# A tuned matmul with bias and tanh: the opening's loads in order of need, and the work of the first row tiles reordered

## The chip, the cores and the metric

One core of one Trainium2 chip. The metric is the time of one execution in microseconds (us), as the median of several runs. The span of a profiled execution is about 1.7 us shorter than its time (1780.2 us of 1781.94 for the kernel before).

## The reference

```python
def reference(a, b, bias):          # a, b: 4096 x 4096 float32; bias: 4096 float32
    return np.tanh(np.matmul(a, b) + bias)
```

## The kernel before

A row tile is 128 rows of A, a k-tile 128 of the inner dimension. A and B are cast to float16 as GpSimd's loads bring them in; TensorE multiplies 128 x 128 by 128 x 512. After a start the kernel runs as a plain loop in which TensorE never waits. The start is special, because A and B have to arrive while TensorE already works: eight row tiles (the first four are `g0`, the second four `g1`) are done together on parts of K, and partial sums are put aside in SBUF (`spill`) and added to later.

The opening (cut):

```python
fill(WARM, NB)                        # dummy matmuls on zeros, WARM = 11
raw_b = spill[3]...                   # float32 landing place of B's k-tiles 0 and 1
for t, copy in enumerate((nc.scalar.copy, nc.vector.tensor_copy)):
    load_b_low(nc.sync, raw_b[:, ds(t, 1), :], 0, t, 1)      # SyncE, 512 KB each
    copy(b_cur[0][:, t, :], raw_b[:, t, :])                  # rounding to float16
...
for m in g0:
    load_nat(m)                       # GpSimd: 128 x 512 of A, turned by TensorE
...
load_b_next()                         # B's k-tiles 2 and 3, GpSimd
load_b_next()
turn_nat(0, nc.vector.tensor_copy)    # four transposes and a copy out of PSUM
fill(3, P)
turn_nat(1, nc.scalar.copy)
row(0, 0, 2)                          # row tile 0, k-tiles 0 and 1: four matmuls
turn_nat(2, nc.vector.tensor_copy)
row(1, 0, 2)
...
```

The later loads are kept in a list and issued by GpSimd in this order, as far as three buffers for A allow (cut):

```python
want_a("g1a", 2, 4 * P, 2 * Q, 0, BL)      # row tiles 4, 5, k-tiles 0..3: four 64 KB loads
want_a("g1a2", 2, 6 * P, 2 * Q, 0, BL)     # row tiles 6, 7
want_a("g1b", G, 4 * P, G * Q, BL, BL)     # row tiles 4..7, k-tiles 4..7
for i in range(BL):
    want(load_b_next)                      # B's k-tiles 4..7
want_a("g0b", G, 0, G * Q, BL, BL)         # row tiles 0..3, k-tiles 4..7
want_a("g0c", G, 0, G * Q, KS, KM - KS)    # row tiles 0..3, k-tiles 8..15
...
```

And the end of the start, where the second four row tiles are finished and the first four take up their second half of K:

```python
for t in (KM, KM + 8):
    for i in range(G):
        turn(ats[G + i], ("g1", t), i * Q, t, 8)      # VectorE transposes
    for m in g1 if t == KM else g0:
        for j in range(J):
            add_bias(m, j)                            # VectorE, eight adds
    across(ps, g1, t, min(t + 8, KT - TB), KS)
turn(ats[0], ("g0", 0), 0, KM, KT - KM)               # row tile 0's second half
down(ps, g1, KT - TB, KT, end)                        # eight final adds, tanh, store
...
for m in g0:
    for j in range(J):
        ...                                           # 16 matmuls
        if m < G - 1 and j == 0:
            turn(ats[m + 1], ("g0", m + 1), 0, KM, KT - KM)
        ...
        end(ps, m, j)
```

## Time and profile before

| | before |
|---|---|
| time, median of 3 runs | 1781.81 us (1781.77 to 1782.02) |
| span of the profiled run | 1780.2 us |
| TensorE busy | 1774.4 us |
| first useful matmul | 7.44 us |
| start of the second four row tiles | 14.80 us |
| row tile 0's second half of K on VectorE | 85.07 us |
| plain loop starts (chain of waits) | 119.10 us |

How to read it: from 119.10 us on TensorE runs without a gap until the last 3.5 us. Whatever a change in the start does to that one number goes into the time one to one, and a load that comes late costs nothing as long as TensorE finds its data. The prediction below shows the lines.

### The profile page before, as it was taken

The page shows a single profiled execution, that of the slowest core. Times are in us where ns is not written, and L with a number is a line of the kernel's source. Part 1 is how long each engine was busy: PE and PEld are TensorE (multiplying, and loading weights), DVE is VectorE, ACT ScalarE, POOL GpSimd, SP SyncE. Part 2 cuts the span into 40 slices and gives each one's busy share as a digit, 9 for nine tenths or more (in the row PEclk, how much of TensorE's full clock was granted, in tenths as well). Part 3 has the DMA queues.
Part 4 walks back from the last instruction along what each step waited for, and adds up shares of the span by engine and source line. Part 5 has one row for each costly group of instructions (what it writes and reads, how often), then busy time and mean ns, then how long its engine had stood idle before and what let it go on. Part 6 is the DMA issues. An engine that isn't in the chain of part 4 may idle for free.

```text
span 1780.2 us, 20854 instructions
## 1 busy us (share of the span) xinstructions
PE 1774.4 (100%) x8254; PEld 806.9 (45%) x8254; DVE 763.8 (43%) x680; ACT 173.2 (10%) x279; POOL 872.1 (49%) x1618
## 2 busy tenths in 40 slices
PE   9999999999999999999999999999999999999999
PEld 4444444444444444444444444444444444444444
DVE  3764353444344443444344443444344443444342
ACT  2011000000000000000000000000000000000001
POOL 7465566544466554444456554444544454444510
PEclk9999999999999999999999999999999999999999
DMA  9999999976999877767699987766776667766641
GB/s 186 203 189 178 168 166 169 140 124 109 165 165 173 148 115 115 119 114 121 113 177 165 170 137 115 119 115 109 129 117 120 107 114 115 120 114 109 116 77 42
DMA packets 281393, 238.94 MB, mean 134 GB/s; under 512 B 159056, under 2 KB 231760, under 8 KB 281296
## 3 DMA queue, kind: packets, MB, share of 16 engines
q0 software_dynamic: 243280, 167.88, 70.1%
q1 hardware_dynamic: 37728, 69.62, 11.0%
q8 instruction: 64, 1.05, 0.2%
q14 instruction: 33, 0.27, 0.0%
q10 hardware_dynamic: 288, 0.13, 0.0%
HBM read 337.64 MB, written 67.11 MB: 227 GB/s over the span
## 4 chain that ended last, share of the span: by engine, by line
PE 99%; DMA 0%; issue 0%; ACT 0%; POOL 0%; DVE 0%; DVEq 0%; POOLq 0%
PE ps L412 93%; PE ps L138 6%; DMA nat<-in_a_dram 0%; ACT o_sb L152 0%; PE tp L257 0%; POOL nat L246 0%; DVE o_sb L149 0%; DVEq L149 0%; POOLq L435 0%
## 5 line engine op out<-in xcount | busy, mean ns | idle before, releaser
L412 PE MATMUL ps<-b,at 128*128 128x512 f16 x7712 | 1657.8, 378 | 0.0
L90 POOL DMA_DIRECT2D an<-in_a_dram x1492 | 805.5, 547 | 796.6 <-DVE at L100 583.4
L412 PEld LDWEIGHTS <-at 128*128 128x128 f16 x7712 | 754.6, 98 | 903.3
L100 DVE STREAM_TRANSPOSE at<-an 128x512 f16<-128x512 f16 (+1 forms) x380 | 565.6, 1539 | 85.8 <-DMA an<-in_a_dram 85.8
L149 DVE TENSOR_TENSOR o_sb<-ps,bias_bc 128x512 f32<-128x512 f32 (+1 forms) x243 | 165.4, 683 | 897.7 <-PE ps L412 695.7
L152 ACT ACTIVATE o_sb<-o_sb 128x512 f32<-128x512 f32 (+1 forms) x243 | 151.8, 626 | 1499.1 <-DVE o_sb L149 1499.1
L73 POOL DMA_DIRECT2D b<-in_b_dram x104 | 56.2, 544 | 15.5 <-DMA an<-in_a_dram 8.4
L138 PE MATMUL ps<-b,atx 128*128 128x512 f16 x256 | 56.2, 379 | 0.0
L138 PE MATMUL ps<-b,at 128*128 128x512 f16 x256 | 55.7, 379 | 0.1
L138 PEld LDWEIGHTS <-at 128*128 128x128 f16 x256 | 25.0, 98 | 30.5 <-DVE spill L181 0.5
L138 PEld LDWEIGHTS <-atx 128*128 128x128 f16 x256 | 24.6, 98 | 30.1 <-DVE atx L100 0.9
L100 DVE STREAM_TRANSPOSE atx<-an 128x512 f16<-128x512 f16 (+2 forms) x12 | 16.3, 1399 | 13.0 <-DMA an<-in_a_dram 13.0
L69 POOL DMA_DIRECT2D b<-in_b_dram x12 | 7.8, 654 | 22.4 <-PE ps L412 22.3
L152 ACT ACTIVATE spill<-spill 128x512 f32<-128x512 f32 x16 | 9.9, 632 | 85.6 <-DVE spill L149 85.5
L149 DVE TENSOR_TENSOR spill<-ps,spill 128x512 f32<-128x512 f32 x16 | 10.4, 678 | 9.9 <-PE ps L138 9.9
L181 DVE TENSOR_TENSOR spill<-spill,bias_bc 128x512 f32<-128x512 f32 x16 | 9.7, 680 | 0.0
L173 ACT COPY spill<-ps 128x512 f32<-128x512 f32 x16 | 8.0, 623 | 12.9 <-PE ps L138 12.9
L228 PE MATMUL ps<-zeros 128*128 128x512 f16 (+1 forms) x14 | 4.7, 498 | 1.3 <-DVE zeros L221 1.3
L176 DVE TENSOR_TENSOR spill<-ps,spill 128x512 f32<-128x512 f32 x8 | 4.8, 670 | 0.0
L228 PEld LDWEIGHTS <-zeros 128*128 128x128 f16 x14 | 1.6, 130 | 3.7 <-issue 2.4
L239 DVE CAST b<-spill 128x1024 f16<-128x1024 f32 x1 | 0.8, 849 | 4.5 <-DMA spill<-in_b_dram 4.5
L246 POOL DMA_DIRECT2D nat<-in_a_dram x4 | 2.3, 587 | 0.8 <-POOLq L435 0.8
(14 smaller groups left out, 8.9 us busy)
## 6 DMA issues: line engine op xcount, KB each, us to landing
an<-in_a_dram POOLq DMA_DIRECT2D x480, 192.0 KB, 5.1
out_dram<-o_sb SPq DMA_DIRECT2D x239, 256.0 KB, 2.7
an<-in_a_dram POOLq DMA_DIRECT2D x960, 32.0 KB, 2.7
b<-in_b_dram POOLq DMA_DIRECT2D x94, 256.0 KB, 8.2
b<-in_b_dram POOLq DMA_DIRECT2D x6, 1024.0 KB, 13.5
an<-in_a_dram POOLq DMA_DIRECT2D x32, 128.0 KB, 5.6
out_dram<-spill SPq DMA_DIRECT2D x16, 256.0 KB, 5.9
an<-in_a_dram POOLq DMA_DIRECT2D x12, 256.0 KB, 8.2
```

The source lines that it names most:

```text
L69: queue.dma_start(out=dst, in_=src[:, ds(t0 % BL, nt), :])
L73: nc.gpsimd.dma_start(out=bt[t0 // TB][ds(q * QP, QP), ds(t0 % TB, nt), :], in_=src.rearrange("(t p) n -> p t n", p=QP),)
L90: nc.gpsimd.dma_start(out=an[ds(q * QP, QP), :, ds((t - t0) * QP, n * QP)], in_=src.rearrange("(mb p) k -> p mb k", p=QP),)
L100: nc.vector.transpose(at[:, ds(t, n), :].rearrange("P t (mb p) -> P mb t p", p=QP), an[:, ds(mb0, Q), ds((t - t0) * QP, n * QP)].rearrange ...
L138: nc.tensor.matmul(ps, at[:, t, :], bt[t // TB][:, t % TB, ts(j, NB)], start=start, stop=stop)
L149: nc.vector.tensor_tensor(out=o_sb[:, piece], in0=ps[:, piece], in1=addend[:, piece], op=mybir.AluOpType.add)
L152: nc.scalar.activation(o_sb[:, piece], o_sb[:, piece], mybir.ActivationFunctionType.Tanh)
L173: nc.scalar.copy(aside(m, j), ps)
L176: nc.vector.tensor_tensor(out=aside(m, j), in0=ps, in1=aside(m, j), op=mybir.AluOpType.add)
L181: nc.vector.tensor_tensor(out=aside(m, j), in0=aside(m, j), in1=bias_bc[:, ts(j, NB)], op=mybir.AluOpType.add)
L228: nc.tensor.matmul(ps[:, ds(0, w)], zeros[:, :P], zeros[:, :w], start=i == 0, stop=i == n - 1)
L412: nc.tensor.matmul(ps, at[:, t, :], b_cur[t // TB][:, t % TB, ds(c0, w)], start=t == 0, stop=t == KT - 1,)
```

## The change

The intent: load first what TensorE needs first, so that the useful work starts earlier, and take VectorE's bias adds out of places where transposes are wanted. It has four parts, which I call the opening, the halves, the pairs and the adds. In the opening, the memset writes into the landing place of B's second k-tile, so SyncE's load of that tile has to wait for it, and it stands behind three loads on GpSimd. I call this the hold.

```diff
# the opening
-    WARM = 11
+    WARM = 9
-    for t, copy in enumerate((nc.scalar.copy, nc.vector.tensor_copy)):
-        load_b_low(nc.sync, raw_b[:, ds(t, 1), :], 0, t, 1)
-        copy(b_cur[0][:, t, :], raw_b[:, t, :])
+    load_b_low(nc.sync, raw_b[:, ds(0, 1), :], 0, 0, 1)
+    for j, copy in enumerate((nc.scalar.copy, nc.vector.tensor_copy)):
+        copy(b_cur[0][:, 0, ts(j, NB)], raw_b[:, 0, ts(j, NB)])
...   (copies of the transposed tiles out of PSUM in two halves each)
-    for m in g0:
+    for m in range(3):
         load_nat(m)
+    nc.gpsimd.memset(raw_b[:, 1, ds(0, 1)], 0.0)      # holds the next load back
+    load_b_low(nc.sync, raw_b[:, ds(1, 1), :], 0, 1, 1)
+    load_nat(3)
...
-    row(0, 0, 2)
+    nc.vector.tensor_copy(b_cur[0][:, 1, :], raw_b[:, 1, :])
+    row(0, 0, 1)
+    row(1, 0, 1)
+    fill(2, P)
     turn_nat(2, nc.vector.tensor_copy)
-    row(1, 0, 2)
+    row(0, 1, 1)
+    row(1, 1, 1)
# the halves
-    want_a("g0c", G, 0, G * Q, KS, KM - KS)
-    for u in range(KS, KM, 2):
-        want(lambda u=u: load_b_all(u, 2))
+    for t in (KS, KS + 4):
+        want_a(("g0", t), G, 0, G * Q, t, 4)
+        for u in (t, t + 2):
+            want(lambda u=u: load_b_all(u, 2))
# the pairs: B's k-tiles 16..19 and 24..27 by two and not by four, the bias load
# after B's k-tiles 24..27 and not before B's 16                     (cut)
# the adds
-        for m in g1 if t == KM else g0:
-            for j in range(J):
-                add_bias(m, j)
         across(ps, g1, t, min(t + 8, KT - TB), KS)
+    for m in g1:
+        for j in range(J):
+            add_bias(m, j)
     turn(ats[0], ("g0", 0), 0, KM, KT - KM)
     down(ps, g1, KT - TB, KT, end)
+    for m in g0:
+        for j in range(J):
+            add_bias(m, j)
```

More of the change, by code (lines that the diff above doesn't have):

```diff
@@ L257, in turn_nat @@
             nc.tensor.transpose(tp[:, t, :], nats[m][:, :, t], ident)
-        copy(ats[m][:, ds(0, BL), :], tp)
+        for t in range(0, BL, 2):
+            copy(ats[m][:, ds(t, 2), :], tp[:, ds(t, 2), :])
     nats, b_done = {}, [2]
-    for m in g0:
+    for m in range(3):
         load_nat(m)
+    nc.gpsimd.memset(raw_b[:, 1, ds(0, 1)], 0.0)
+    load_b_low(nc.sync, raw_b[:, ds(1, 1), :], 0, 1, 1)
+    load_nat(3)
     nc.gpsimd.affine_select(
@@ L300 @@
     bias_bc = biasp.tile([P, NCW], fp32, name="bias_bc")
-    want(lambda: load_bias(bias_bc, 0, nc.gpsimd))
     for t in (KM, KM + 8):
         want_a(("g1", t), G, 4 * P, G * Q, t, 8)
-        for u in range(t, t + 8, TB):
-            want(lambda u=u: load_b_all(u, TB))
+        for u in (t, t + 2):
+            want(lambda u=u: load_b_all(u, 2))
+        if t > KM:
+            want(lambda: load_bias(bias_bc, 0, nc.gpsimd))
+        want(lambda t=t: load_b_all(t + TB, TB))
     for m in g0:
@@ L325 @@
     ps = {}
-    for m in g0:
-        turn(ats[m], "g0c", m * Q, KS, KM - KS)
+    for t in (KS, KS + 4):
+        for m in g0:
+            turn(ats[m], ("g0", t), m * Q, t, 4)
     one_by_one(ps, g0, BL, KS, BL)
@@ L343 @@
             turn(ats[G + i], ("g1", t), i * Q, t, 8)
-        for m in g1 if t == KM else g0:
-            for j in range(J):
-                add_bias(m, j)
         across(ps, g1, t, min(t + 8, KT - TB), KS)
+    for m in g1:
+        for j in range(J):
+            add_bias(m, j)
     turn(ats[0], ("g0", 0), 0, KM, KT - KM)
     down(ps, g1, KT - TB, KT, end)
+    for m in g0:
+        for j in range(J):
+            add_bias(m, j)
     ahead = 3
```

## The prediction

> **What bounds the kernel now.** I read the page first, for the span and the busy shares; then the chain that ended last in order of time, for where TensorE's stream begins and breaks; then the timelines of single engines around the places that the change touches.
>
> The page of the kernel before, its first lines and a line of its chain:
>
> ```profile
> span 1780.2 us, 20854 instructions
> PE 1774.4 (100%) x8254; PEld 806.9 (45%) x8254; DVE 763.8 (43%) x680; ACT 173.2 (10%) x279; POOL 872.1 (49%) x1618
> ...
> PE 99%; DMA 0%; issue 0%; ACT 0%; POOL 0%; DVE 0%; DVEq 0%; POOLq 0%
> ```
>
> TensorE is the bound, but a busy share of 100% alone doesn't say that it runs at its pace, because matmuls are pipelined. A long stretch in the middle does, in the view by windows:
>
> ```profile
> 1000.00:1700.00 700.00, 700.00 (x3245) 317.38 (x3244) 297.82 (x254) 63.78 (x101) 328.91 (x614) 1.00 0.72 119
> ```
>
> 700 us over 3245 matmuls is 0.2157 us each, and there are 4096 x 4096 x 4096 / (128 x 128 x 512) = 8192 of that size: 8192 x 0.2157 = 1767 us that no ordering of loads changes. Of the span of 1780.2 only about 13 us are open to anything, and the chain in order of time shows where they lie:
>
> ```profile
> 7.11 0.05 issue
> 7.16 0.42 PE tp L257 x4
> 7.58 0.90 PE ps L138 x4
> 8.48 0.22 PE tp L257 x4
> 8.70 0.86 PE ps L138 x4
> 9.56 0.22 PE tp L257 x4
> 9.79 25.99 PE ps L138 x120
> 35.78 0.05 issue
> 35.82 41.60 PE ps L138 x192
> 77.42 0.08 issue
> 77.50 41.60 PE ps L138 x192
> 119.10 1654.20 PE ps L412 x7680
> ```
>
> The first useful matmul starts at 7.44 us, the transposes between rows cost 0.22 each, and afterwards the stream is without gaps but for 0.05 and 0.08 us. 120 x 0.2157 = 25.9 against 25.99, 192 x 0.2157 = 41.4 against 41.60. So all that the change can win is in the first 7.4 us, and every stall that it makes later is paid in full. The last 3.5 us (a last add, tanh and store) are not touched.
>
> Two later places have little slack. In VectorE's timeline, at 28 us and at 85 to 101 us:
>
> ```profile
> 27.93 2.50 DVE L100 STREAM_TRANSPOSE atx<-an 128x512 f16<-128x512 f16 x4 [6.30 <-DMA an<-in_a_dram]
> ...
> 46.16 2.37 DVE L100 STREAM_TRANSPOSE at<-an 128x1024 f16<-128x1024 f16 x2 [8.22 <-DMA an<-in_a_dram]
> 48.46 4.84 DVE L176 TENSOR_TENSOR spill<-ps,spill 128x512 f32<-128x512 f32 x8
> ```
>
> ```profile
> 85.07 2.31 DVE L100 STREAM_TRANSPOSE atx<-an 128x2048 f16<-128x2048 f16 x1 [3.85 <-DMA an<-in_a_dram]
> 87.31 4.90 DVE L149 TENSOR_TENSOR spill<-ps,spill 128x512 f32<-128x512 f32 x8
> 92.12 2.30 DVE L100 STREAM_TRANSPOSE atx<-an 128x2048 f16<-128x2048 f16 x1
> 94.97 0.69 DVE L149 TENSOR_TENSOR spill<-ps,spill 128x512 f32<-128x512 f32 x1 [0.55 <-PE ps L138]
> 98.42 0.69 DVE L149 TENSOR_TENSOR spill<-ps,spill 128x512 f32<-128x512 f32 x1 [2.76 <-PE ps L138]
> ```
>
> Look at the transpose at 92.12: it makes the second half of K for row tile 1 and ends at 94.42. TensorE starts row tile 0's second half at 91.31 and needs 32 matmuls, 32 x 0.2157 = 6.9 us, so it wants row tile 1 at 98.2. Slack: 3.8 us.
>
> **What the Trainium skill says.** "TensorE: Matmul & The Clock Gate", section "Wait — 56ns, not 53.3ns?", gives 215.7 ns between starts of warm 512-column matmuls; the trace has 0.2157 us, so the stream is at its pace. The same page, section "What's actually happening", has the array at half clock until it was busy for a free-running window of about 3.4 us. The trace agrees: the filling matmuls take 0.42 us each from 1.26 us on and become quick just before 5 us. "DMA: Bandwidth & Descriptors", section "Issuing engines are not separate DMA queues", says that loads from all issuing engines run on the same 16 DMA engines and interleave. The trace agrees in effect: the first row tile's load is issued at 1.31 and lands at 6.5, 5.2 us later, while two float32 tiles of B of 512 KB pass. "Trace Analysis" (its title in full: "Perfetto Trace Analysis"), section "Tensor Engine Instruction (MATMUL, LD_WEIGHTS)", says VectorE takes its instructions in strict order; that matters for the largest term below, and VectorE's timeline shows nothing against it.
>
> **The change part by part.**
>
> *Start.* The row tiles no longer queue behind both tiles of B. 512 KB at the 409 GB/s that the view by windows has from 4 to 5 us is 1.3 us, so the first row tile should land at about 5.2 instead of 6.5. TensorE needs two row tiles before its first row (both sets of transposes come first in its order), and the second lands between 5.9 and 7.1, by whether B's second tile, whose first bytes I expect at about 4.3 (GpSimd's memset behind three issues of 0.55 us, then the issue and its latency of about 1 us), goes ahead of it. Four matmuls can then run on B's first tile. The second must land, and be rounded by VectorE in 0.85 us: about 7.2 to 8.4. Counted as a stream without gaps, TensorE is 0 to 0.9 us ahead of before. With WARM 9 the fills still reach to about 5.0 us, so the clock should open as before. The memset is 0.1 us on GpSimd. The split PSUM copies add an instruction each (0.42 us becomes perhaps 2 x 0.27) but release the first half sooner: about nothing.
>
> *What becomes of it.* At 28.7 TensorE takes up A's k-tiles 4 to 7 of the first four row tiles. Their load landed at 27.93 and the first of four transposes takes 0.68, so ready at 28.6: no slack. The DMA queue is full from 2.5 us to there, and neither bytes nor their order after B's tile 3 change in this stretch. So TensorE arrives earlier and waits: the 0 to 0.9 us go to this wait. Net 0.
>
> *The load of A's k-tiles 8 to 15 in two halves.* Rows of 256 bytes in place of 512. By the trace's packets, 2048 of 256 bytes take about 3.0 us, and 2048 of 512 bytes 5.3 us, so 2 x 3.0 - 5.3 = 0.7 us more DMA time, and all later loads land so much later. The halves themselves have room: the first lands near 31 and is wanted at 35.8, the second near 39 and is wanted at 42.7. The load for 46.16 moves to 46.8, its two transposes end at 49.2, and the eight adds that free PSUM start then, not at 48.46; TensorE wants the first bank at 49.63 and would get it at 49.9: a stall of 0.3 us, which the larger one below swallows.
>
> *B's k-tiles 16, 18, 24 and 26 in pairs and the bias load later.* More issues on GpSimd (8 times 0.55 us), which is 49% busy, and the same bytes. Bias comes before B's last tiles instead of before A's. About 0 for what lands last.
>
> *The bias adds of the first four row tiles.* This is the term that counts. Before, eight adds of line 181 lay at 76.36 to 81.22, where VectorE then waited 3.85 us for a load. Now they come after the eight adds that finish the second four row tiles and ahead of the transpose for row tile 1 (the compiled order of VectorE says so). They wait for nothing and take (81.22 - 76.36) / 8 = 0.61 us each, 4.86 for eight. So in place of the transpose at 92.12:
>
> - with the loads as before: adds of line 149 end at 92.2, bias adds at 97.05, transpose 2.30, at 99.35. TensorE wanted it at 98.2, plus about 0.05 for the signal: 1.2 us of stall;
> - with the loads 0.65 later: row tile 0's transpose starts at 85.7, the eight adds behind it (not paced by TensorE, but by VectorE) end at 92.85, bias adds at 97.7, transpose at 100.0: 1.9 us;
> - at least: the last add of line 149 can't start before TensorE ends the stage at 91.3, so it ends at 92.0, and the transpose at 99.1: 0.95 us.
>
> This is an absolute time on VectorE: what TensorE wins or loses before 98 us hardly changes it. Afterwards the stream has room again. The transposes of row tiles 2 and 3 have 3 us and more, and the next row's load, issued at 99.6 in place of 94.7, lands at about 113 (it took 13.3 us before), for a transpose at about 114.
>
> *Sum.* Start 0, wait at 28.7 included; stall at 49.6 0.3, swallowed; stall at 98 between 0.95 and 1.9, middle 1.5. 1781.8 + 1.5 = 1783.3 us.
>
> **Rivals.** First, the gain at the start survives: loads land earlier throughout, and the bias adds don't hurt. Then about 1781.0. For it: fewer bytes ahead of the first row tile, and a queue that GpSimd fills in better order. Against it: the zero slack at 28.7 with a full queue, and the order of VectorE, where 2.30 + 4.86 us come after 91.3 + 0.7 = 92.0. Second, the clock: nine fills end before a window does, the rows run on half a clock for up to 3.4 us. That adds up to 1.7 us at the start, which the wait at 28.7 has not the slack to absorb, but the VectorE chain at 98 would hide in part; 1783.5 to 1785. Against it: the clock opens just before 5 us, and the fills still reach there. Third, B's tiles 28 to 31, wanted at 84.2, land late: before they landed near 82.5, and 0.7 later is still in time; if the smaller loads leave the queue dry for a microsecond or two, another microsecond: 1784 to 1785.
>
> **Range and chances.** The middle of the first term gives 1783.3. A chain without any slip downwards gives 1782.7, and a little gain in the load stream 1782.3; the late loads and the clock give 1784.8. So 1782.2 to 1784.8. Two per cent is 35.6 us, and no stage that is touched is large enough: faster 0.005, same 0.985, slower 0.01.
>
> **What would show each step.** The first useful matmul between 6.0 and 7.5 us; a wait of TensorE near 28.7 as long as the lead; VectorE's eight adds of line 181 starting at 92 to 93 and the transpose behind them ending at 99 to 100.3; a gap in TensorE's chain of 1 to 2 us there; the number of matmuls after it at the same pace. The prediction is wrong if TensorE has no gap at 98, which means that the transpose came in time, or if the wait at 28.7 is missing and the whole load stream has moved earlier.

## The result, and the profile after

| | before | after |
|---|---|---|
| median of the same rounds | 1781.91 us (1781.77 to 1782.03) | 1787.59 us (1786.95 to 1788.49) |
| span of the profiled run | 1780.2 us | 1786.2 us |
| ratio after to before | | 1.0032 (95%: 1.0015 to 1.005) |

A ratio is the mean time of one kernel's fast runs over the mean of the other's of the same rounds, so it isn't quite the ratio of the medians. By the verdict's 2% the two are the same; but the change costs 5.7 us where 1.5 were predicted, and the time lies outside the predicted range (1782.2 to 1784.8). The class was right and the size wrong.

The page of the kernel after, its first line and the shares of the chain that ended last:

```profile
span 1786.2 us, 20886 instructions
...
PE 94%; DMA 4%; POOL 1%; DVE 1%; issue 1%; ACT 0%; DVEq 0%; POOLq 0%
```

Before, the chain was 99% TensorE. Now DMA has 4%: the chain runs back through loads for the first hundred microseconds. The chain of the kernel after in order of time (start, duration, what) says which:

```profile
4.51 8.49 DMA b<-in_b_dram
...
13.29 3.12 POOL an L90 x5
...
28.50 5.41 DMA an<-in_a_dram
...
75.55 7.48 DMA bias_bc<-in_bias_dram
...
83.32 6.58 DMA an<-in_a_dram
90.03 2.32 DVE atx L100
...
98.82 3.09 DVE spill L181 x5
101.91 2.23 DVE atx L100
104.19 20.89 PE ps L138 x96
125.08 1654.20 PE ps L428 x7680
```

Read it from the end. The plain loop (`L428`) starts at 125.08, 5.98 us after the 119.10 of before, and takes the same 1654.20. TensorE takes up row tile 1's second half at 104.19, as VectorE's transpose of it (`atx L100` at 101.91) ends. Ahead of that transpose stand the eight moved bias adds (`L181`), ahead of them eight final adds and the transpose of row tile 0 at 90.03, which waited for a load. The first lines show where lateness began: GpSimd (POOL) could issue five loads of A only at 13.29, because a load of B that it had issued at 4.51 had to land first. The bias load, which the pairs moved, is a link too: GpSimd issued row tile 0's load at 83.32, after the bias had landed. It is one in every traced run that has the pairs and waits at row tile 1, but no run takes the pairs out alone, so what this link costs isn't known.

TensorE's timeline of the kernel after; the bracket is the idle time just before and what ended it:

```profile
8.11 0.61 PE L257 MATMUL tp<-ident,nat 128*128 128x128 f16 x4 [2.39 <-DMA nat<-in_a_dram]
8.52 1.91 PE L138 MATMUL ps<-b,atx 128*128 128x512 f16 x4
...
17.22 13.98 PE L138 MATMUL ps<-b,at 128*128 128x512 f16 x64
31.83 20.89 PE L138 MATMUL ps<-b,atx 128*128 128x512 f16 x96 [0.64 <-DVE atx L100]
53.63 41.60 PE L138 MATMUL ps<-b,at 128*128 128x512 f16 x192 [0.91 <-DVE spill L176]
...
104.19 20.89 PE L138 MATMUL ps<-b,atx 128*128 128x512 f16 x96 [2.05 <-DVE atx L100]
```

The second four row tiles start at 17.22, 2.42 us later than before; row tile 0's second half starts at 95.07 (before 91.31), 3.76 later; the plain loop 5.98 later. So the losses lie in three places, two of which the prediction held to be zero. Look also at 8.52: four matmuls took 1.91 us, where four took 1.04 in the kernel before. TensorE ran at half clock there. The wait of 2.39 us ahead of it, for the second row tile, is new.

### The profile page after: what moved, and what is told of

Its sections match the earlier page's. It is cut to its first block, busy times and chain, and to the rows that moved or that the text cites. A ratio compares the mean times of both kernels' runs of the same rounds, so it can differ in the third digit from the quotient of the medians.

```text
span 1786.2 us, 20886 instructions
## 1 busy us (share of the span) xinstructions
PE 1775.2 (99%) x8254; PEld 807.5 (45%) x8254; DVE 764.4 (43%) x687; ACT 172.5 (10%) x281; POOL 875.4 (49%) x1631
## 4 chain that ended last, share of the span: by engine, by line
PE 94%; DMA 4%; POOL 1%; DVE 1%; issue 1%; ACT 0%; DVEq 0%; POOLq 0%
PE ps L428 93%; DMA an<-in_a_dram 2%; DMA b<-in_b_dram 1%; PE ps L138 1%; POOL an L90 1%; DMA bias_bc<-in_bias_dram 0%; DVE atx L100 0%; DVE spill L181 0%; POOL b L73 0%; POOL nat L246 0%; POOL b L69 0%; DVE spill L149 0%; ACT o_sb L152 0%; DVE o_sb L149 0%; POOL ident L268 0%
## 5 line engine op out<-in xcount | busy, mean ns | idle before, releaser
L428 PE MATMUL ps<-b,at 128*128 128x512 f16 x7712 | 1657.8, 378 | 0.0
L428 PEld LDWEIGHTS <-at 128*128 128x128 f16 x7712 | 754.6, 98 | 903.3
L100 DVE STREAM_TRANSPOSE at<-an 128x512 f16<-128x512 f16 (+1 forms) x380 | 565.6, 1539 | 94.1 <-DMA an<-in_a_dram 94.1
L73 POOL DMA_DIRECT2D b<-in_b_dram x112 | 60.2, 541 | 11.7 <-DMA an<-in_a_dram 6.8
L138 PEld LDWEIGHTS <-at 128*128 128x128 f16 x256 | 25.1, 98 | 31.2 <-issue 1.2
L100 DVE STREAM_TRANSPOSE atx<-an 128x512 f16<-128x512 f16 (+1 forms) x16 | 16.7, 1086 | 15.1 <-DMA an<-in_a_dram 15.1
L69 POOL DMA_DIRECT2D b<-in_b_dram x12 | 7.8, 660 | 15.7 <-PE ps L428 15.4
L181 DVE TENSOR_TENSOR spill<-spill,bias_bc 128x512 f32<-128x512 f32 x16 | 9.8, 685 | 3.7 <-DMA bias_bc<-in_bias_dram 3.7
L173 ACT COPY spill<-ps 128x512 f32<-128x512 f32 x16 | 8.0, 624 | 12.8 <-PE ps L138 12.8
```

The lines of the kernel that those rows point to most:

```text
L69: queue.dma_start(out=dst, in_=src[:, ds(t0 % BL, nt), :])
L73: nc.gpsimd.dma_start(out=bt[t0 // TB][ds(q * QP, QP), ds(t0 % TB, nt), :], in_=src.rearrange("(t p) n -> p t n", p=QP),)
L100: nc.vector.transpose(at[:, ds(t, n), :].rearrange("P t (mb p) -> P mb t p", p=QP), an[:, ds(mb0, Q), ds((t - t0) * QP, n * QP)].rearrange ...
L138: nc.tensor.matmul(ps, at[:, t, :], bt[t // TB][:, t % TB, ts(j, NB)], start=start, stop=stop)
L173: nc.scalar.copy(aside(m, j), ps)
L181: nc.vector.tensor_tensor(out=aside(m, j), in0=aside(m, j), in1=bias_bc[:, ts(j, NB)], op=mybir.AluOpType.add)
```

## The experiments

My theory after the first reading: the held-back load of B makes the whole stream of loads late, and VectorE's chain behind row tile 0's load carries that lateness into the time. The rivals: two queues share the engines badly, whatever the order; the other new parts of the opening are at fault; the 5.7 us are a sum of separate stalls, the half clock among them. Kernels are compared only within the same rounds. Every run is the same as before at 2%. The intervals of after, e2, e5 and e8 lie above 1 (e4's begins at 1.0), those of all other runs hold 1: smaller differences of medians lean on one trace each. "The engines' share" is the DMA share in the view by windows, the time of the packets over that of 16 engines; it goes above 1 where packets overlap.

### The parts alone

**e1_opening_only**: the kernel before with the opening of the diff, nothing else.

> The kernel before with only the opening of the change (second tile of B held back, first tile rounded by two engines, rows reordered, PSUM copies in halves, nine fills). Theory 1 (the held-back load mixes with the row tiles on the same 16 DMA engines, lands them late, and the whole load stream is then 2 to 3 us late): the load that the kernel before waits for at 27.93 lands at 31.0 +- 0.4, TensorE is 3 us late from there on, and no stall is added at 98, so 1785.0 (1784.3 to 1785.6). Rival (the stream is late because of the later parts of the change, the opening costs nothing, as the prediction had it): 1781.9 +- 0.4.

Measured: 1783.43 us (1783.07 to 1785.42) against 1782.07, ratio 1.0010 (0.9994 to 1.0027). Between the two theories. The second four row tiles start at 15.24; TensorE then waits 0.50 us at 29.7 for A's k-tiles 4 to 7, which are turned from 28.95 on (before 27.93); no stall near 98.

**e2_rest_only**: the kernel before with the halves, the pairs and the adds, without the opening.

> The kernel before with all of the change but its opening. Theory 1: the load before row tile 0's second half (85.07 before) lands about 2 us later, at 87, and the chain of VectorE behind it (2.3 + 4.84 + 4.84 + 2.3 us) ends at 101.3 where TensorE wants it at 98.2: 1785.0 (1784 to 1785.8). The prediction's own sum: that load at 85.7, 1783.7. Rival (all is the opening): 1781.9.

Measured: 1784.66 us (1784.21 to 1787.36) against 1782.07, ratio 1.0017 (1.0002 to 1.0032). Its timeline of VectorE:

```profile
85.93 2.31 DVE L100 STREAM_TRANSPOSE atx<-an 128x2048 f16<-128x2048 f16 x1 [2.18 <-DMA an<-in_a_dram]
...
92.92 4.89 DVE L181 TENSOR_TENSOR spill<-spill,bias_bc 128x512 f32<-128x512 f32 x8
97.73 2.31 DVE L100 STREAM_TRANSPOSE atx<-an 128x2048 f16<-128x2048 f16 x1
```

The prediction had worked out 85.7 for the first line, 92.85 for the start of the bias adds and 97.7 for the second transpose. TensorE then waits once, 2.25 us, up to 100.09. With the opening left out, the steps of the prediction after the opening come out almost to the tenth in this trace, and its span is 1.9 us over before's. It is the fastest of the four runs, though; the median is 2.6 us over before, above the prediction's own sum (1783.7) and in theory 1's range, although the load came at 85.93 and not at theory 1's 87.

**e3_adds_only**: only the bias adds moved.

> The kernel before with only the bias adds moved behind the stage's last adds. The prediction's term: the transpose of row tile 1 ends at 99.35 and not at 94.42, TensorE waits 1.2 us at 98.2: 1783.0 (1782.7 to 1783.3). Rival (the adds hide): 1781.9.

Measured: 1784.00 us (1783.01 to 1784.25) against 1782.07, ratio 1.0009 (0.9994 to 1.0024). In its trace the wait ahead of row tile 1 is 0.91 us, and there are three more of 0.41, 0.19 and 0.30 us at earlier places (29.4, 50.7 and 78.7 us). The first is close to the smallest of the three cases that the prediction gave (0.95), but not by that case's working: row tile 0's load came at 86.29, the transpose ended at 100.48, and TensorE was itself late by the other waits. The time is 1 us above the expectation. Up to 29 us this kernel does the same as the one before, yet A's k-tiles 4 to 7 came at 28.60 and not at 27.93: so much one trace can differ from another.

**e17_opening_no_hold**: the opening without the hold-back (both tiles of B issued at once), on the kernel before.

```diff
     load_b_low(nc.sync, raw_b[:, ds(0, 1), :], 0, 0, 1)
+    load_b_low(nc.sync, raw_b[:, ds(1, 1), :], 0, 1, 1)
...
-    nc.gpsimd.memset(raw_b[:, 1, ds(0, 1)], 0.0)
-    load_b_low(nc.sync, raw_b[:, ds(1, 1), :], 0, 1, 1)
```

> The kernel before with all of the opening but the hold-back (nine fills, B's first tile rounded in halves, copies in halves, rows in the new order). Theory: the load stream is as before, A's k-tiles 4 to 7 land at 27.9 +- 0.4 and the DMA share from 14 to 16 us is above 1.5; time 1781.7 to 1782.5 if the clock opens in time. Rival (the other parts of the opening cost the microsecond that the opening alone cost): 1783.0 to 1784.0. A half clock up to 9.7 us would show in the clock record and add at most 1 us at the start of the second four rows.

Measured: 1783.15 us (1782.62 to 1783.77) against 1782.57, ratio 1.0003 (0.999 to 1.0016). A's k-tiles 4 to 7 at 27.74, the engines' share from 14 to 16 us 1.52: the load stream is in time, as the theory has it. The time lies in the rival's range (1783.0 to 1784.0): TensorE waits 0.81 us at 78.2. Its runs overlap with those of e1, so the two times alone don't show what the hold costs within the opening.

**e16_hold_only**: nothing but the hold-back on the kernel before, with eleven fills and whole rows.

> The kernel before with nothing but the hold-back: B's second k-tile is issued on SyncE after three row tiles, eleven fills and whole rows as before. Theory (the held-back load by itself makes the opening's load stream late): the row tiles' median issue to landing rises from 5.2 to above 6 us, the DMA engines' share from 14 to 16 us falls from 1.62 to below 1.1, A's k-tiles 4 to 7 land after 29.2 us instead of 27.93, and TensorE's second four rows start after 15.6 instead of 14.80; time 1783.0 to 1784.2. Rival (the lateness comes of the nine fills, the half clock and the order of the rows, the hold is only along): load at 27.9 +- 0.4, time 1781.8 to 1782.4.

Measured: 1784.66 us (1783.52 to 1785.81) against 1782.57, ratio 1.0011 (0.9998 to 1.0023). Its timeline of TensorE:

```profile
8.08 0.41 PE L256 MATMUL tp<-ident,nat 128*128 128x128 f16 x4 [1.60 <-DMA nat<-in_a_dram]
...
10.86 1.91 PE L138 MATMUL ps<-b,atx 128*128 128x512 f16 x4
...
18.06 13.98 PE L138 MATMUL ps<-b,at 128*128 128x512 f16 x64
```

The hold alone makes the hole, then the half clock (1.91 us for four matmuls), and puts the second four row tiles at 18.06, 3.26 us later than before. The loads are late too, but less than the theory said: A's k-tiles 4 to 7 at 28.83 (29.2 was expected), the share from 14 to 16 us 1.29 (below 1.1 was expected). The time is above the theory's range (1783.0 to 1784.2). The rival falls: the hold isn't merely along, and no run here is as fast as any of the kernel before.

### The whole change with one thing undone

**e4_no_hold**: the changed kernel without the hold-back, by the same edit as in e17.

> The changed kernel, but both tiles of B issued at once on SyncE as before; all else of the change stays. Theory 1: the load stream is as in e2, so the same time as e2 (about 1785.0) and about 2.5 us less than the changed kernel's 1787.6; the loads of row tiles land at 6.5, 7.2, 7.8, 8.4 as before. Rival (the lateness comes from another part of the opening, such as the row order, the split copies or the clock): as the changed kernel, 1787.6.

Measured: 1784.83 us (1783.89 to 1785.86) against 1782.07, ratio 1.0015 (1.0 to 1.0029). It is 2.8 us over before instead of 5.7, as theory 1 had it. A's k-tiles 4 to 7 come at 28.05, row tile 0's second half at 87.27. The clock opened only at 9.68 us in its profiled run, so the second four row tiles started at 15.98.

**e8_after_again**: the changed kernel, repeated on another chip.

> The changed kernel once more, on the same chip as the next three, because the held-back load cost 1.2 us alone (e1) and seemed to cost 2.8 us in the whole change (changed kernel against e4), and those were different chips. If that is a matter of chip or run, 1786 to 1787 here, with the load of 28 us (31.06 in its first trace) at 29 to 30; if the parts add more than singly, 1787.6 again.

Measured: 1786.44 us (1785.33 to 1786.94) against 1782.41, ratio 1.0022 (1.0007 to 1.0037): 4.0 us over before here. The trace has the same pattern, half clock from 7.58 to 10.99, row tile 0's second half at 88.59, the last wait 1.34 us.

**e5_one_queue**: B's second tile through GpSimd's queue in place of SyncE's, without the memset, in the same place of the order.

```diff
-    nc.gpsimd.memset(raw_b[:, 1, ds(0, 1)], 0.0)
-    load_b_low(nc.sync, raw_b[:, ds(1, 1), :], 0, 1, 1)
+    load_b_low(nc.gpsimd, b_cur[0][:, ds(1, 1), :], 0, 1, 1)
```

> The changed kernel, but B's second tile is issued by GpSimd in the same place of its own queue (after three row tiles, converted on the way, so no memset and no rounding) and not by SyncE. The order of need stays, the second queue goes. Theory 1a (what costs is that two queues share the 16 DMA engines packet by packet, so that every load in flight lands late and GpSimd, which keeps 8 loads in flight, issues later): row tiles land at about 5.2, 5.9, 6.5, 8.5, B's tiles 2 and 3 at about 10 and 11.2 as before, and the time falls to that of the change without its opening (e2, e4), 1784.8 +- 0.7. Theory 1b (what costs is the order, B's second tile behind three row tiles): no gain, 1786 to 1788.

Measured: 1786.61 us (1785.73 to 1788.09) against 1782.41, ratio 1.0027 (1.001 to 1.0044). The second row tile now lands early (its transposes run at 6.07, not 8.11), but B's second tile comes at 9.01, and the later loads are nearly as late as with two queues: 29.23 and 87.75 (30.03 and 88.59 in e8). The time is in theory 1b's range. Two queues that mix aren't needed to make the stream late; the order is enough.

**e9_one_queue_alone**: the same one-queue opening on the kernel before, with eleven fills.

> The kernel before with only that opening in one queue, and eleven fills. The first row starts at about 6.2 to 6.5 (7.44 before), B's second tile lands at 7.7. Theory: the lead is eaten by the wait for the load that lands at about 27.9, so the same as before, 1781.9 +- 0.4. Rival (the lead survives): 1781.1.

Measured: 1783.31 us (1782.76 to 1784.39) against 1782.41, ratio 1.0006 (0.9991 to 1.0021). The engines' share from 14 to 16 us is 0.84, A's k-tiles 4 to 7 come at 30.48, and TensorE waits 0.44 us at 24.8 and 1.07 us at 31.2. Both expected times miss: the first row starts at 6.97 (6.2 to 6.5 expected), but B's second tile lands at 9.11 (7.7 expected), and the second four row tiles start 0.6 us later than before.

### Why a late B tile makes everything after it late

GpSimd's timeline before:

```profile
11.21 3.12 POOL L90 DMA_DIRECT2D an<-in_a_dram  x5 [0.68 <-DMA b<-in_b_dram]
14.32 2.17 POOL L69 DMA_DIRECT2D b<-in_b_dram  x4
```

and after:

```profile
13.29 3.12 POOL L90 DMA_DIRECT2D an<-in_a_dram  x5 [0.68 <-DMA b<-in_b_dram]
16.39 2.18 POOL L69 DMA_DIRECT2D b<-in_b_dram  x4
```

Both issue the same loads in the same order. Counted through from the start, GpSimd has at most eight loads under way; the ninth issue waits until the first load has landed, and so on. Whether the chip or the program sets this number isn't shown. B's k-tile 3, issued at 4.5 us, landed at 10.9 before and at 13.0 after, and the group behind it moves by 2.08 us, and so does all that follows. This group of five is a good mark for the state of the stream:

| kernels | start of the group of five |
|---|---|
| both tiles of B at once: before, e2, e3, e4, e17 | 11.21, 11.45, 11.64, 11.26, 11.46 us |
| second tile held back: after, e8, e1, e16, e13, e19, e20 | 13.29, 13.54, 12.38, 12.61, 12.74, 13.47, 11.91 us |

No run of the one kind reaches the other; the means are 11.4 and 12.8 us. Also, the loads under way were too small to keep the engines busy: eight loads of 64 KB (row tiles 4 to 7) fill most of the places. The view by windows, from 14 to 16 us (the last two numbers are the DMA share and GB/s), in the kernel before:

```profile
14.00:16.00 2.00, 2.00 (x11) 0.91 (x10) 1.30 (x2) 2.00 (x6) 2.00 (x5) 1.00 1.62 156
```

and after:

```profile
14.00:16.00 2.00, 2.00 (x11) 0.94 (x10) 1.30 (x2) 0.09 (x1) 2.00 (x4) 1.00 0.75 69
```

156 GB/s became 69: after the late landing the engines have run nearly dry. That asks for an experiment on the size of the loads.

**e12_one_load**: the changed kernel, with row tiles 4 to 7 in one load of four 128 KB pieces.

```diff
-    want_a("g1a", 2, 4 * P, 2 * Q, 0, BL)
-    want_a("g1a2", 2, 6 * P, 2 * Q, 0, BL)
+    want_a("g1a", G, 4 * P, G * Q, 0, BL)
```

> The changed kernel, with the first load of A for the second four row tiles in 4 issues of 128 KB in place of 8 of 64 KB (as in e10). Theory 2 (the opening's lateness grows because GpSimd keeps 8 loads in flight, each issue waiting for the landing of the one 8 before, and runs dry at 13 to 15 us): the DMA engines stay busy there (0.69 to 0.75 in 14 to 16 us before this edit, 1.5 or more with it), the load of 30 to 31 us lands at or before 29, and the time falls by 1.5 to 2.5, to 1784.3 +- 0.7. What is left is TensorE's late and half-clocked first rows and the bias adds. Rival (the bandwidth itself is lost, whatever the issue): 1786 to 1787.6.

Measured: 1783.88 us (1783.59 to 1784.69) against 1782.62, ratio 1.0009 (0.9994 to 1.0024). The share from 14 to 16 us is 1.81 with 178 GB/s, A's k-tiles 4 to 7 come at 26.34 in place of 31.06 and 30.03, row tile 0's second half at 85.71, and one wait is left after the opening, 1.28 us. The same bytes in half as many loads take back 3.7 to 4.7 us of load time and most of the loss. In this profiled run the opening's loads were also less late (B's k-tile 3 at 11.63) and the clock stayed up; but in e14, with the same loads, B's k-tile 3 came at 12.85 and A's k-tiles 4 to 7 still at 26.73.

**e10_one_load**: the same on e9.

> As e9, and the first load of A for the second four row tiles is made in 4 issues of 128 KB in place of 8 of 64 KB, so that the 8 loads in flight cover more bytes and GpSimd's issue comes 4 x 0.58 us earlier; the trace of before has the DMA engines partly dry at 13 to 14 and 16.5 to 19. Theory (the load stream is held back by the 8 loads in flight): the load of 27.93 lands 0.5 to 1.5 us earlier, the lead survives, 1781.1 (1780.7 to 1781.6). Rival (bandwidth alone): 1781.9.

Measured: 1782.64 us (1782.5 to 1783.1) against 1782.41, ratio 1.0002 (0.9987 to 1.0017). Share 1.81 instead of 0.84, load at 26.82 instead of 30.48. The larger load is whole only at 15.07, though, so TensorE waits 0.80 us at 15.85, and the lead doesn't survive: the time is above both that were expected.

**e11_merge_only**: the same on the kernel before.

> The kernel before with g1a and g1a2 in one load of four 128 KB pieces instead of eight of 64 KB. The engines' share from 14 to 16 us rises from 1.62 to about 1.8 and the load of A's k-tiles 4 to 7 lands at 25 to 26.5 instead of 27.93. The stream of TensorE has no gap in the kernel before that an earlier load could close, so theory: 1781.6 to 1782.4, no gain. Rival (earlier loads also take away the 0.05 to 0.08 us gaps and the run to run spread): 1781.3 and a smaller spread than before's.

Measured: 1781.54 us (1781.51 to 1781.63, 5 runs) against 1782.57 (1781.70 to 1783.49, 9 runs), ratio 0.9994 (0.998 to 1.0008). All five runs lie below all nine of the kernel before. The median is 0.06 us below the theory's range, and the spread is small, as the rival had it: "no gap" in the kernel before wasn't quite true. TensorE's timeline of before has at 28.7 and 49.6

```profile
28.70 21.10 PE L138 MATMUL ps<-b,atx 128*128 128x512 f16 x96
49.63 41.84 PE L138 MATMUL ps<-b,at 128*128 128x512 f16 x192
```

where e11's has

```profile
28.77 20.88 PE L138 MATMUL ps<-b,atx 128*128 128x512 f16 x96
49.49 41.60 PE L138 MATMUL ps<-b,at 128*128 128x512 f16 x192
```

0.22 and 0.24 us of small pauses have gone with the earlier loads (25.70 in place of 27.93), together what the span lost (1780.2 to 1779.8). That the earlier loads also explain the narrower spread fits, but no slower run of the kernel before was traced.

### Does VectorE's chain set the end?

If row tile 0's load and VectorE's fixed work behind it set the end, then TensorE takes up row tile 1 a fixed time after that load, whatever happened before, and the span is fixed with it. Every profiled run that waits there:

| run | row tile 0 on VectorE | TensorE at row tile 1 | difference | span |
|---|---|---|---|---|
| after | 90.03 | 104.19 | 14.16 | 1786.2 |
| e8_after_again | 88.59 | 102.75 | 14.16 | 1784.8 |
| e5_one_queue | 87.75 | 101.91 | 14.16 | 1784.0 |
| e19_after_filled | 87.74 | 101.90 | 14.16 | 1783.9 |
| e4_no_hold | 87.27 | 101.43 | 14.16 | 1783.4 |
| e3_adds_only | 86.29 | 100.53 | 14.24 | 1782.5 |
| e2_rest_only | 85.93 | 100.09 | 14.16 | 1782.1 |
| e12_one_load | 85.71 | 99.87 | 14.16 | 1781.9 |

The difference stays at 14.16 us (14.24 in e3, where the eight final adds took 4.91 us in place of 4.84), and the span is 1682.0 us more than the third column. So in these traces one number decides, the time of that load. What decides that load is another question (see e19).

**e13_adds_spread**: the changed kernel, but each bias add of the first four row tiles directly ahead of its final add, so that none stands ahead of row tile 1's transpose.

```diff
     down(ps, g1, KT - TB, KT, end)
-    for m in g0:
-        for j in range(J):
-            add_bias(m, j)
...
+            add_bias(m, j)
             end(ps, m, j)
```

> The changed kernel, with the eight bias adds of the first four row tiles each just ahead of the add that ends its tile, not in a row ahead of row tile 1's transpose. The prediction's step (VectorE's chain sets the time there): the transpose ends 4.84 us earlier, TensorE no longer waits there (2.05 us in the changed kernel's first trace, 1.34 in its second), 1785.3 +- 0.6. Rival (the wait only moves to another place): 1786.5 to 1787.6.

Measured: 1783.99 us (1783.1 to 1784.42) against 1782.62, ratio 1.0008 (0.9993 to 1.0023). The time is below the theory's range (1784.7 to 1785.9). Row tile 0's load is still late, 88.43, and there is no wait: TensorE's stream across the place is one piece,

```profile
93.40 27.79 PE L138 MATMUL ps<-b,atx 128*128 128x512 f16 x128
```

What is left of the loss is the late start (second four row tiles at 16.50) and one wait of 0.51 us at 52.0.

**e14_both**: e12 and e13 together.

> Both edits. If the time is what is left of TensorE's late start (second row tile lands at 8.1 to 8.3 and not 7.16, first rows at half clock), the first matmul of the second four row tiles at 16.5 to 17.2 in place of 14.8 and no further wait: 1783.9 +- 0.6. If waits for loads come back elsewhere: 1785 or more.

Measured: 1782.96 us (1782.19 to 1783.6) against 1782.62, ratio 1.0002 (0.9986 to 1.0019). It is below the theory's range (1783.3 to 1784.5). No wait after 17 us; the second four row tiles start at 16.57, and that alone is left.

### The half clock

The clock record of every run moves in windows of 3.41 us. The view by windows for the kernel after, with the first full-speed window and the one behind it (TensorE's busy time is the second number, the granted clock the one before the last two):

```profile
4.21:7.62 3.41, 1.19 (x10) 0.51 (x8) 0.92 (x3) 0.62 (x1) 2.62 (x5) 1.00 1.08 246
7.62:11.03 3.41, 2.92 (x15) 1.75 (x16) 0.69 (x1) 0.65 (x2) 1.35 (x3) 0.50 1.18 200
```

The hole in front of the second row tile left 1.19 us of work in the first, and the second ran at half clock. In three other traces the first full-speed window had as little work, 1.22 us (e8), 1.41 us (e16) and 1.61 us (e13), and in each the next one ran at half clock. In all others it had 2.00 us or more (2.00 in e14, 2.03 in e12, 2.43 in before), and the clock stayed. Where the windows lie differs from trace to trace: in the four kernels with the opening of before, the clock opened at 4.43, 4.92, 6.11 and 6.23 us. So the same hole can count differently: e13's second row tile came at 7.11, no later than e12's at 7.17, but e13's window kept 1.61 us of work and e12's 2.03.

What closed the clock again in these four is the empty time behind the fills, as e16 shows with eleven; with the hole filled it stays open (e20 and e19, below). Nine fills can cost in another way, as e4 shows without the hold: they end at 5.28, the window from 2.86 to 6.27 us has 2.45 us of work, and the clock opens only at 9.68.

**e20_hold_filled**: e16 with the hole filled by eight dummy matmuls of 512 columns (`fill(8, NB)` in place of `fill(3, P)`).

> The hold-back alone on the kernel before, with eight dummy matmuls of 512 columns in the hole of 1.60 us instead of three of 128. Here no bias adds stand ahead of a row tile on VectorE. Theory (the hold costs twice, by a late load stream that this kernel can absorb in part, and by the half clock that follows the hole): no window at half clock, second four rows at 16.2 to 16.8 us instead of 18.06, time 1782.9 to 1783.8 against 1784.66 for the hold alone. Rival (the late loads are all of it): 1784.3 to 1785.0 with TensorE waiting near 29 us.

Measured: 1783.73 us (1782.82 to 1786.08) against 1782.81, ratio 1.0007 (0.9994 to 1.0019): 0.9 us over before, where the hold without the filling was 2.1 over; the runs of the two overlap, so this gain isn't clear of noise. No window at half clock, the second four row tiles at 16.04 in place of 18.06 (16.2 to 16.8 expected). The theory's range holds the median. What remains is late loads; the profiled run waits 1.28 us at 79.6 for B.

**e19_after_filled**: the changed kernel with its hole filled by ten (`fill(10, NB)`).

> The changed kernel with TensorE's hole between the first and the second row tile (2.39 us in its trace) filled by ten dummy matmuls of 512 columns instead of three of 128. Both theories: the clock record shows no window at half speed after the opening, and TensorE's second four rows start at 15.5 to 16.2 us instead of 17.22. Theory (the end is an absolute time, set by the late load of row tile 0 and VectorE's chain behind it): the time stays at 1786.0 to 1787.8, and the wait near 100 us grows to 3 us or more from 2.05. Rival (the half clock is a loss that passes to the end): 1784.9 to 1785.9.

Measured: 1784.68 us (1784.58 to 1786.49) against 1782.81, ratio 1.0013 (0.9999 to 1.0026). The median is below both ranges, by 1.3 us for the theory and by 0.2 for the rival; the five runs lie on both sides of the rival's range, so the rival isn't refuted. No half clock, the second four row tiles at 16.79, not the 15.5 to 16.2 that was expected: the second row tile is as late as before (8.06), and short waits for the third (0.22 us) and for B's second tile (0.23 us) follow. The wait at row tile 1 did not grow, it fell to 1.18 us, since row tile 0's load came at 87.74 in place of 90.03 or 88.59. The row in the table above says that the end still hangs on that load. But the load doesn't stand apart from TensorE. The chain of this trace, in order of time, has

```profile
11.78 39.55 PE ps L138 x183
...
52.68 3.41 DVE spill L176 x6
...
58.54 2.34 DVE at L100 x2
...
61.10 1.91 POOL an L90 x3
```

TensorE's own work leads up to 51.33 us, then VectorE's adds and transposes, and only then GpSimd issues the loads of A that lead on to row tile 0's. In the trace of after, GpSimd and the loads made the chain up to 90.03, but for one transpose at 34.04. So TensorE's late start can make that load late. How much of the gain of 0.9 to 2.3 us is owed to the filling stays open: up to the group of five (13.47) the stream is as late as in the two others, and the two traces of the changed kernel differ by 1.4 us themselves.

### A better version

**e15_start**: e11, with row tile 0's first k-tile put ahead of row tile 1's transposes, so that TensorE starts with one row tile.

```diff
     fill(3, P)
-    turn_nat(1, nc.scalar.copy)
-    row(0, 0, 2)
+    row(0, 0, 1)
+    turn_nat(1, nc.scalar.copy)
+    row(0, 1, 1)
     turn_nat(2, nc.vector.tensor_copy)
     row(1, 0, 2)
```

> A version meant to beat both: the kernel before, with the same 4 issues in place of 8 (which gives the load that lands at 27.93 about 1 us of room), and row 0's first k-tile ahead of row tile 1's transposes. First useful matmul at about 7.0 in place of 7.44, and the room lets 0.3 us of it survive: 1781.5 (1781.2 to 1781.9) where the kernel before has 1781.8. If the one load lands too late for its first use (14.8), 1782 to 1782.6.

Measured: 1781.91 us (1781.84 to 1782.0) against 1782.62, ratio 0.9997 (0.9982 to 1.0012). The first useful matmul came at 7.57 us, not at 7.0.

**e18_start_again**: the same kernel in more rounds.

> The kernel of e15_start unchanged, in more rounds. Theory: it starts TensorE's rows no earlier than before and has no gap, so it is the same as before within 0.3 us: 1781.7 to 1782.2. Rival (it is really faster, as its earlier loads and its narrower spread suggest): ratio with the interval below 1.

Measured: 1781.86 us (1781.60 to 1782.26) against 1782.57, ratio 0.9996 (0.9983 to 1.0009), in the theory's range. The row order gains nothing over e11 (1781.54), so the larger load alone is the best version found: 1.0 us below before at the medians.

## Why the prediction was wrong where it was, and right where it was

- **Start** failed. "TensorE is 0 to 0.9 us ahead of before": it was 2.42 us behind at the second four row tiles. The first row tile came as predicted (its transposes at 5.14). The second was to land "between 5.9 and 7.1" and came at 8.1, B's second tile was to be there and rounded at 7.2 to 8.4 and landed at 9.80, though it was issued at 3.20. I had given B's second tile its bytes at the engines' best rate (1.3 us), as if nothing shared them.
- **The clock** was named as the second rival, with 1783.5 to 1785, but by another mechanism ("nine fills end before a window does"), which only e4's trace shows. In the kernel after, the clock did open early, at 4.21, and closed again behind the hole that the hold makes (e16 has it without the other parts; with the hole filled, in e20 and e19, it stayed open). I had followed the window only up to its opening, and by one trace.
- **"What becomes of it ... neither bytes nor their order after B's tile 3 change in this stretch ... Net 0"** is the step that cost most: with the loads brought forward in e12, 1.3 us of the loss were left. Bytes and order were indeed the same; their times were not. B's k-tile 3 landed 2.1 us later, and GpSimd's later issues wait for such landings: A's k-tiles 4 to 7 came at 31.06 in place of 27.93. The prediction also took the DMA queue for full from 2.5 us on; the view by windows of the kernel before has 201 GB/s from 6 to 8 us, but 108 from 16 to 18. I treated the stream as a rate, where it is also a chain: the group of five (11.2 to 11.6 us without the hold, 11.9 to 13.5 with it) shows it.
- **The halves: +0.7 us** isn't shown. Row tile 0's load came at 85.93 in e2 (85.7 predicted), but at 86.29 in e3, which has no halves, and no run has the halves alone. In the whole change it came at 90.03: the mis-sized term, by 4.3 us.
- **The bias adds** were right in mechanism. "This is an absolute time on VectorE" is what the table of eight runs shows; 14.3 us were predicted from that load to TensorE's restart, 14.16 measured. The stall in e2 was 2.25 us (1.9 predicted for late loads; TensorE came there 0.5 us earlier). Taking the adds away takes the wait away (e13).
- **Sum.** Put the measured 90.03 for the predicted 85.7 into the working for late loads, and 1781.8 + 1.9 + 4.3 gives 1788.0 us; the traced run took 1787.91, the median is 1787.59. At the end of such a chain the earlier losses aren't added once more; they can only act through the load at its start.
- **What would make it wrong** was given as no gap at 98 or an earlier stream. The gap was there (2.05 us), but the first useful matmul came at 8.52 (6.0 to 7.5 expected) and VectorE's eight adds at 97.03 (92 to 93). That the stream could move later was in none of the rivals; the third rival came nearest ("if the smaller loads leave the queue dry for a microsecond or two"), but blamed other loads and allowed one microsecond.

Open remain three things. First, why B's tiles 2 and 3 land later when B's second tile is loaded behind the row tiles: in one queue or two it happens, and the traces don't show which load's pieces an engine takes first. Second, why the size of that delay varies so: the group of five starts 0.5 to 2.1 us after the mean of the kernels without the hold. Its cost varies with it: the opening alone cost 1.4 us in e1, the hold alone 2.1 in e16, and the hold within the whole change 1.2 to 2.9 us (5.7 and 4.0 less the 2.8 of e4). Third, how the delay of row tile 0's load divides: between the late stream, TensorE's late start (e19), and the halves and pairs with the bias load, which no run has alone.

## What to carry to other kernels

Ordering loads by need didn't pay here, because the landings behind them moved: the issuing engine waits for old loads, so a load put behind others delayed the issue of everything later, and small loads used up the places. Before moving work on an engine, look for the chain with an absolute end (here one load and 14.16 us of VectorE) and ask what the change does to its first link. And a wait put into TensorE's warm-up may cost a whole window at half clock on top.

## What the Trainium skill lacked or had wrong

- "TensorE: Matmul & The Clock Gate", section "What's actually happening", has the array fall back "after ≥1 idle window". Here a window needn't be idle: first full-speed windows of 3.41 us with 1.19, 1.22, 1.41 and 1.61 us of work were followed by one at half clock, those with 2.00 us and more were not. The length of the window agrees (3.41 us in the clock records).
- "DMA: Bandwidth & Descriptors", section "Issuing engines are not separate DMA queues", says that loads interleave whatever engine issued them, and e5 agrees (one queue, loads nearly as late: 29.23 us against 30.03). That section doesn't warn that a load moved behind others can delay those that were issued at the same time as before: B's k-tile 3 landed at 13.0 in place of 10.9 us.
- No page read for this has how many loads GpSimd has under way before it waits for a landing. These traces show eight (whether the chip or the program sets it isn't shown). With 64 KB pieces the share from 14 to 16 us was 1.62 with 156 GB/s before and 0.75 with 69 after, with 128 KB pieces 1.81 with 179 (e11) and 178 (e12).
